# Four seven-product pairs in every gate-and-up group, and bank sums added by transfers

## The chip, the cores and the metric

The kernel runs on one core of one Trainium2 chip. The metric is the device time of one execution in microseconds (us), the median of three runs. The engines are PE (TensorE, matmul; its weight loads are PEld), DVE (VectorE), ACT (ScalarE), POOL (GpSimd) and SP (SyncE, which issues most DMA transfers). Each engine works through its own queue in a fixed order; an instruction that waits holds up what stands behind it on its engine. PE writes to PSUM, eight banks of 128 x 512 fp32; the other memory on the chip is SBUF. A transfer that accumulates reads its destination, adds, and writes it back.

## The reference

One residual block on x of 256 rows and 2048 columns in fp32: a feed-forward half step, a mixing part (gated DeltaNet and attention), and a second feed-forward half step. The change touches only the first two matrix products of both feed-forward parts:

```
def swiglu(h, w_gate, w_up, w_down):
    return (jax.nn.silu(h @ w_gate) * (h @ w_up)) @ w_down

x = x + 0.5 * swiglu(rms_norm(x, ffn1_norm), ffn1_w_gate, ffn1_w_up, ffn1_w_down)
# ... mixing: projections, DeltaNet and attention, gated merge ...
x = x + 0.5 * swiglu(rms_norm(x, ffn2_norm), ffn2_w_gate, ffn2_w_up, ffn2_w_down)
```

Here h is 256 x 2048, w_gate and w_up are 2048 x 5504 and w_down is 5504 x 2048.

## The kernel before

**Precision.** Every fp32 operand is split into a high part (rounded, a cast on ACT) and a low part (the rest, a subtraction on DVE). A product is three matmuls into one bank: high by high, high by low, low by high (`product`, L454 to L456). So each weight tile costs ACT a cast and DVE a subtraction (names `wh`, `wl`; L372 and L426).

**Groups.** The 43 column tiles of the hidden dimension are worked in 11 groups of four tiles (512 columns), the last of three (384). A group is named by its first tile c = 0, 4, ... 40. Eight pairs j = 0 to 7 of 128-row blocks of h are run for each group (`seven`, L480), and give four results: gate and up for both halves of the rows. The groups form three chunks, `CHUNKS`: c = 0 to 12, 16 to 28, 32 to 40. After a chunk comes its down stage, which adds the chunk's part of the third matrix product to x; in the first two chunks this, too, uses seven products for some pairs (`DEEP`).

**Plain and fast pairs.** A plain pair is eight products, 24 matmuls, into four banks: 2, 4, 3, 8. A fast pair computes the same eight from seven products (a Winograd form), 21 matmuls, into seven banks; for it, DVE first forms four combinations of the weight blocks (`s`, L398 to L400), and these are split like weights (`sh`, `sl`), beside two weight blocks `w` and one, `v`. After the last fast pair of a group the seven banks are combined in SBUF into four sums `ev` (tiles `ef`; a copy at L523 and four additions, L524 to L527). The plain banks, which went on collecting, are added to these sums at the end of the group:

```
        for b in (2, 3, 4, 8):
            nc.vector.tensor_add(ev[b], banks[b], ev[b])
```

(L539). Then come SiLU on the two gate sums (ACT, L555) and the product with the two up sums (DVE, L557).

**Which pairs are fast.** FFN 1's group 0 has none. The first two groups of each chunk have four, `FOUR` = 0, 2, 4, 6; the others have three, `FAST` = 0, 2, 4.

**Hidden jobs.** A group's result is transposed on PE (L137) and split (L127 on ACT, L128 on DVE) as two jobs in the following group. In the second to fourth groups of the first two chunks a job may also form the sums for the down stage (tiles `shid`, `hs`; L574, L144 to L147). Jobs are run between plain pairs that come late enough after the last fast one; with `FAST` that is from pair 6 on, with `FOUR` all are left to the end of pair 7.

**Order.** The kernel is written as one program; a scheduler then fixes each engine's order. Weights are fetched by SP some pairs ahead into a heap of 22 SBUF buffers, rounded and split up to a few pairs ahead of PE. Accumulating transfers exist already: the down stage adds its sums to x in DRAM from POOL's queue (L601).

Of the kernel before, what the change touches and what calls it, by code (L numbers as in the profile page):

```python
# [11 lines left out]
F32 = mybir.dt.float32  # L12
F32R = mybir.dt.float32r
AF = mybir.ActivationFunctionType
ALU = mybir.AluOpType
AX = mybir.AxisListType

P = 128
T = 256
D = 2048  # L20
KD = D // P
# [5 lines left out]
BIG = 1e30  # L27
NB = 22
NH = 2
FAST = (0, 2, 4)  # L30
FOUR = (0, 2, 4, 6)
DOWN = (2, 4, 6)
DEEP = (2, 3, 5, 6)
# [2 lines left out]
CHUNKS = ((0, 4), (4, 8), (8, 11))  # L36
# [5 lines left out]
def block_kernel(ctx: ExitStack, tc: tile.TileContext, a: dict, out: bass.AP):  # L42
# [5 lines left out]
    nc = tc.nc  # L48
# [9 lines left out]
    def heap(shape, dt, name):  # L58
        return hp.tile(shape, dt, tag="h", name=name)
# [56 lines left out]
    def tick():  # L116
        for job in later:
            job[0] -= 1
        while later and later[0][0] <= 0:
            later.popleft()[1]()  # L120
# [144 lines left out]
    def fast_pairs(f, i):  # L265
        if f == "1" and i == 0:
            return ()
        return FOUR if any(a0 <= i < a0 + 2 for a0, _ in CHUNKS) else FAST

    def pairs_of(f, i):  # L270
        return FIRST if f == "1" and i == 0 else range(KD // 2)
# [4 lines left out]
    def plan():  # L276

        for f in "12":
            for a0, a1 in CHUNKS:
                for i in range(a0, a1):  # L280
                    c, m = FG[i]
                    js = pairs_of(f, i)
                    gu = zip(*(t_pieces(a[w + f], c, m, 0, KD, [2 * j for j in js]) for w in ("wg", "wu")))
                    for j, p in zip(js, gu):
                        yield j in fast_pairs(f, i), p
                k0, k1 = FG[a0][0], sum(FG[a1 - 1])
                cols = lambda d: t_pieces(a["wd" + f], 4 * d, 4, k0, k1)
                if down_pairs(a0, a1):
                    for d in (0, 2):
                        yield from sevens(cols(d), cols(d + 1), DEEP)  # L290
                else:
                    for d in range(4):
                        yield from twos(cols(d))
            if f == "2":
                return
            yield from mixing()
# [134 lines left out]
    def take_weights():  # L431
        tick()
        while sum(c for c, _ in ready) <= min(PREP, taken[0]) and (left[0] or begun):
            prepare()
        taken[0] += 1
        return ready.popleft()[1]
# [11 lines left out]
    def product(dst, act, wt, start, stop):  # L448

        (ah, al), (wh, wl) = act, wt  # L450
        dst = dst[:, : int(np.prod(wh.shape[1:]))]
        if len(wh.shape) == 3:
            dst = dst.rearrange("p (c x) -> p c x", x=P)
        nc.tensor.matmul(dst, ah, wh, start=start, stop=False)  # L454
        nc.tensor.matmul(dst, ah, wl, start=False, stop=False)  # L455
        nc.tensor.matmul(dst, al, wh, start=False, stop=stop)  # L456
# [20 lines left out]
    def wide(name, n=512):  # L477
        return tp.tile([P, 512], F32, name=name, tag="w", bufs=8)[:, :n]


    def seven(nm, n, fast, act, jobs=(), feed=None, pairs=range(KD // 2), out=None):

        size = {b: len(fast) for b in range(1, 9)}
        for b in (2, 3, 4, 8):
            size[b] += 2 * (KD // 2 - len(fast))
        size[8] -= len(fast)
        done = dict.fromkeys(size, 0)
        banks = {}  # L490

        def add(b, act, wt):
            if b not in banks:
                banks[b] = (acc_bank if b < 5 else core_bank)(f"p{nm}_{b}")[:, :n]
            done[b] += 1
            product(banks[b], act, wt, done[b] == 1, done[b] == size[b])

        ev = {}
        idle = 0
        for at_pair, j in enumerate(pairs):  # L500
            if j in fast:
                ps = take_weights()
                for at, (b, i7, w) in enumerate(ps):
                    add(b, act(j, i7), w)
                    if at == 3:
                        tick()
            else:
                for s in range(2):
                    wh, wl, _ = take_weights()
                    if feed and s == 0:  # L510
                        feed(at_pair)
                    for k, w in enumerate(zip(wh, wl)):
                        for t in range(2):
                            add((2, 4, 3, 8)[2 * s + t], act(j, 2 * k + t), w)
                    idle += 1
                    if idle > 3 and jobs and j > max(fast, default=-1):
                        jobs.popleft()()
                    while at_pair == KD // 2 - 1 and s == 1 and jobs:
                        jobs.popleft()()
            if fast and j == fast[-1]:  # L520
                idle = 1
                g0, u0, g1, u1 = (wide(f"e{nm}_{x}", n) for x in range(4))
                nc.scalar.copy(g0, banks[1])  # L523
                nc.vector.tensor_add(u0, banks[6], g0)  # L524
                nc.vector.tensor_add(g1, banks[7], u0)
                nc.vector.tensor_add(u1, banks[5], g1)
                nc.vector.tensor_add(u0, banks[5], u0)  # L527
                ev = {2: g0, 3: u0, 4: g1, 8: u1}
        if out:
            for b, put in out.items():  # L530
                put(ev[b])
                e = wide(f"e{nm}_{b}", n)
                nc.scalar.copy(e, banks[b])
                put(e)
            return None
        if not fast:
            return banks
        for b in (2, 3, 4, 8):
            nc.vector.tensor_add(ev[b], banks[b], ev[b])  # L539
        return ev  # L540

    def gate_up(nm, f, i, xr, jobs, feed):

        c, m = FG[i]
        n, fast = m * P, fast_pairs(f, i)
        src = seven(f"f{nm}_{c}", n, fast, xr.sums_of, jobs, feed, pairs_of(f, i))
        if not fast:
            banks = src
            src = {b: wide(f"e{nm}_{c}_{b}", n) for b in QUAD}
            for b in QUAD:  # L550
                (nc.scalar.copy if b % 4 else nc.vector.tensor_copy)(src[b], banks[b])
        gs = [src[b] for b in (2, 4)]
        us = [src[b] for b in (3, 8)]
        for t in range(2):
            nc.scalar.activation(gs[t], src[(2, 4)[t]], AF.Silu, scale=xr.rn[:, t : t + 1])  # L555
        for t in range(2):
            nc.vector.scalar_tensor_tensor(  # L557
                us[t], src[(3, 8)[t]], xr.half_rn[:, t : t + 1], gs[t], op0=ALU.mult, op1=ALU.mult
            )
        return us  # L560

    def ffn(nm, xr, nxt, feed):
# [15 lines left out]
        for a0, a1 in CHUNKS:  # L578
# [18 lines left out]
            if fast:  # L597
                block = lambda j, b: act(2 * j + b // 2, b % 2) if b < 4 else [sums[j][:, s, b - 4] for s in range(2)]
                for d in (0, 2):
                    out = {  # L600
                        b: lambda e, dst=xd[d + dd][t]: nc.gpsimd.dma_start(dst, e, accum_op=ALU.add)  # L601
                        for b, (dd, t) in QUAD.items()
                    }
                    seven(f"d{nm}_{a0}{d}", 512, fast, block, out=out)
                continue
# [21 lines left out]
    def put(xs, d):  # L627
        for t in range(2):
            nc.sync.dma_start(xd[d][t], xs[t])
# [506 lines left out]
    def feed(s):  # L1136

        if s < 7:
            xr1.plain(FIRST[s + 1], pair_of_x(FIRST[s + 1]))
        if s < 6:  # L1140
            load_x(2 * FIRST[s + 2], 2)
        if s == 1:
            nc.sync.dma_start(cst, a["cst"])
        if s == 6:
            nc.sync.dma_start(hd, a["hd"].partition_broadcast(P))
        if s > 1 and FIRST[s] in xr1.fast:
            xr1.more(FIRST[s], pair_of_x(FIRST[s]))
        for k4 in range(4):
            if s == max(3, *(FIRST.index(2 * k4 + i) for i in range(2))):
                stand(k4)  # L1150
        if s == 7:
            xr1.finish()
# [49 lines left out]
    act = xr2.more_again(DOWN)  # L1202
# [116 lines left out]
```

## Time and profile before

| | us |
|---|---|
| median of three runs | 2108.11 (2108.03 to 2108.55) |
| the profiled execution | 2107.68 |
| its span, first to last instruction | 2105.9 |
| PE busy | 2090.3 |
| DVE busy | 1767.7 |
| ACT busy | 1179.4 |
| POOL busy | 64.5 |

Rows of groups give line, engine, operation, output and input tile, shapes and count, then busy time and the mean of one. Rows of a timeline give start, duration, engine, line, operation, tiles, count, and in brackets the idle time before with what ended it. A matmul's row lasts longer than the time until the next one starts, since matmuls overlap. A row by stretch of time gives start and end, the length, then the busy time of PE, PEld, DVE, ACT and POOL with counts, the granted clock, the DMA share and GB/s.

### The profile page before, as it was taken

The numbers are of one execution on the slowest core, as the hardware profiler recorded it, in microseconds if no ns is written. First come the engines' busy times: TensorE is split into PE (matmuls) and PEld (weight loads), VectorE is DVE, ScalarE is ACT, GpSimd is POOL, SyncE is SP. The second block draws the span as 40 slices with busy tenths as digits, with TensorE's granted clock in tenths as the row PEclk, the third lists the DMA queues.
The fourth block names the chain that finished last, engine by engine and source line by source line (L and its number), as shares of the span: only waits on it lengthen the run. The fifth ranks groups of instructions, "written<-read, shape, count | busy, mean of one in ns | idle before, by whom it ended". The sixth has DMA issues, their size and how long they took to land.

```text
span 2105.9 us, 25649 instructions
## 1 busy us (share of the span) xinstructions
PE 2090.3 (99%) x9747; PEld 1746.8 (83%) x9747; DVE 1767.7 (84%) x1959; ACT 1179.4 (56%) x1208; POOL 64.5 (3%) x77
## 2 busy tenths in 40 slices
PE   9999999999999999999999999999999999999999
PEld 6888888878898988888888888888887888878897
DVE  6998999989996788667784787669999999989982
ACT  6755565645655555567555554555555555556561
POOL 0000110002000000000010000000000100011000
PEclk9999999999999999999999999999999999999999
DMA  9655995649866656435454467757665975579581
GB/s 317 219 189 175 262 265 196 205 145 278 253 217 211 237 197 219 164 120 200 145 180 160 142 204 231 234 179 230 202 198 167 280 238 196 180 206 295 186 272 60
DMA packets 398202, 434.57 MB, mean 206 GB/s; under 512 B 14704, under 2 KB 372352, under 8 KB 397824
## 3 DMA queue, kind: packets, MB, share of 16 engines
q1 hardware_dynamic: 388864, 416.17, 60.9%
q0 software_dynamic: 9216, 16.78, 4.5%
q8 instruction: 76, 1.25, 0.2%
q14 instruction: 46, 0.38, 0.1%
HBM read 407.72 MB, written 25.17 MB: 206 GB/s over the span
## 4 chain that ended last, share of the span: by engine, by line
PE 96%; DVE 2%; SPq 1%; issue 0%; DMA 0%; ACT 0%; DVEq 0%; ACTq 0%
PE pf L454 14%; PE pf L456 14%; PE pf L455 14%; PE pd L455 7%; PE pd L456 7%; PE pd L454 7%; PE pg L455 2%; PE pg L456 2%; PE pg L454 2%; PE pc L454 2%; PE pc L456 2%; PE pc L455 2%; PE pwo L456 1%; PE pwo L454 1%; PE pwo L455 1%; DVE wl L426 1%
## 5 line engine op out<-in xcount | busy, mean ns | idle before, releaser
L426 DVE TENSOR_TENSOR wl<-raw,wh 128x2048 fp32r<-128x2048 f32 (+5 forms) x283 | 598.7, 2125 | 70.5 <-PE pc L455 16.9
L372 ACT CAST wh<-raw 128x2048 fp32r<-128x2048 f32 (+5 forms) x283 | 499.9, 1782 | 95.7 <-DVE wl L426 20.5
L405 ACT CAST sh<-s 128x2048 fp32r<-128x2048 f32 (+1 forms) x118 | 223.4, 1893 | 279.5 <-DVE s L400 276.5
L426 DVE TENSOR_TENSOR sl<-s,sh 128x2048 fp32r<-128x2048 f32 (+1 forms) x118 | 265.8, 2258 | 26.8 <-PE pd L455 11.9
L455 PE MATMUL pf<-wl,xr 128*128 128x512 f32 (+1 forms) x704 | 271.4, 386 | 0.0
L456 PE MATMUL pf<-wh,xr 128*128 128x512 f32 (+1 forms) x704 | 271.3, 385 | 0.0
L454 PE MATMUL pf<-wh,xr 128*128 128x512 f32 (+1 forms) x704 | 262.2, 387 | 2.2 <-ACT xr L179 1.5
L456 PE MATMUL pd<-wh,hid 128*128 128x512 f32 x432 | 169.1, 391 | 0.0
L455 PE MATMUL pd<-wl,hid 128*128 128x512 f32 x432 | 168.3, 389 | 0.0
L454 PE MATMUL pd<-wh,hid 128*128 128x512 f32 x432 | 163.6, 392 | 0.0
L403 ACT CAST w<-raw 128x1024 fp32r<-128x1024 f32 (+1 forms) x118 | 122.8, 1040 | 64.7 <-DVE sl L426 12.8
L454 PEld LDWEIGHTS pf<-wh,xr 128*128 128x128 f32 x704 | 132.7, 189 | 28.3 <-ACT xr L179 1.9
L456 PEld LDWEIGHTS pf<-wh,xr 128*128 128x128 f32 x704 | 132.5, 188 | 25.4 <-DVE xr L180 0.2
L455 PEld LDWEIGHTS pf<-wl,xr 128*128 128x128 f32 x704 | 132.6, 188 | 25.2 <-DVE wl L426 0.4
L426 DVE TENSOR_TENSOR w<-raw,w 128x1024 fp32r<-128x1024 f32 (+1 forms) x118 | 142.3, 1206 | 10.1 <-ACT w L403 9.9
L398 DVE TENSOR_TENSOR s<-raw 128x1024 f32<-128x1024 f32 (+1 forms) x118 | 142.1, 1204 | 6.8 <-PE pg L455 4.6
L403 ACT CAST v<-raw 128x512 fp32r<-128x512 f32 (+1 forms) x118 | 72.6, 615 | 91.3 <-PE pf L456 30.9
L455 PE MATMUL pf<-sl,xf 128*128 128x512 f32 (+1 forms) x296 | 113.8, 385 | 0.0
L456 PE MATMUL pf<-sh,xf 128*128 128x512 f32 (+1 forms) x296 | 113.5, 385 | 0.0
L454 PE MATMUL pf<-sh,xf 128*128 128x512 f32 (+1 forms) x296 | 112.0, 386 | 0.0
L601 POOL DMA_DIRECT2D xd<-ed x64 | 56.0, 997 | 1305.7 <-ACT ed L523 1228.1
L456 PEld LDWEIGHTS pd<-wh,hid 128*128 128x128 f32 x432 | 81.1, 188 | 17.2
(472 smaller groups left out, 4247.9 us busy)
## 6 DMA issues: line engine op xcount, KB each, us to landing
raw<-wd SPq DMA_DIRECT2D x168, 512.0 KB, 5.1
raw<-wg SPq DMA_DIRECT2D x159, 512.0 KB, 3.8
raw<-wu SPq DMA_DIRECT2D x159, 512.0 KB, 5.2
raw<-wgt SPq DMA_DIRECT2D x64, 512.0 KB, 4.6
raw<-wa SPq DMA_DIRECT2D x48, 512.0 KB, 4.6
raw<-wc SPq DMA_DIRECT2D x48, 512.0 KB, 4.6
xd<-ed POOLq DMA_DIRECT2D x64, 256.0 KB, 6.9
raw<-wbr SPq DMA_DIRECT2D x32, 512.0 KB, 4.9
```

Of the source, the lines that this page charges most:

```text
L372: nc.scalar.copy(hi, src)
L398: nc.vector.tensor_sub(S[:, 0:2], R[:, 1], R[:, :, 0])
L403: nc.scalar.copy(hi, src)
L405: nc.scalar.copy(sh, s)
L426: nc.vector.tensor_sub(lo, src, f32(hi))
L454: nc.tensor.matmul(dst, ah, wh, start=start, stop=False)
L455: nc.tensor.matmul(dst, ah, wl, start=False, stop=False)
L456: nc.tensor.matmul(dst, al, wh, start=False, stop=stop)
L601: b: lambda e, dst=xd[d + dd][t]: nc.gpsimd.dma_start(dst, e, accum_op=ALU.add)
```

## The change

All groups but FFN 1's group 0 now have four fast pairs. That concerns the third and fourth group of the first two chunks and the last group, ten in all (c = 8, 12, 24, 28, 40 in both FFNs). In all groups with fast pairs but a chunk's last one, the additions of L539 are no longer made: ACT copies the four plain banks into a new SBUF tile `es`, in the order 2, 4, 3, 8, and POOL issues a transfer for each that adds it to the sum `ev`. These are 15 groups: c = 4, 8, 16, 20, 24, 32, 36 in FFN 1 and the same with c = 0 in FFN 2. SiLU and the product with the up sums now follow the transfers.

```diff
-FAST = (0, 2, 4)
 FOUR = (0, 2, 4, 6)
...
         if f == "1" and i == 0:
             return ()
-        return FOUR if any(a0 <= i < a0 + 2 for a0, _ in CHUNKS) else FAST
+        return FOUR
...
-    def seven(nm, n, fast, act, jobs=(), feed=None, pairs=range(KD // 2), out=None):
+    def seven(nm, n, fast, act, jobs=(), feed=None, pairs=range(KD // 2), out=None, spill=False):
...
         if not fast:
             return banks
+        if spill:
+            es = heap([P, 4, n], F32, f"e{nm}")
+            for i, b in enumerate((2, 4, 3, 8)):
+                nc.scalar.copy(es[:, i], banks[b])
+                nc.gpsimd.dma_start(ev[b], es[:, i], accum_op=ALU.add)
+            return ev
         for b in (2, 3, 4, 8):
             nc.vector.tensor_add(ev[b], banks[b], ev[b])
         return ev
...
         n, fast = m * P, fast_pairs(f, i)
-        src = seven(f"f{nm}_{c}", n, fast, xr.sums_of, jobs, feed, pairs_of(f, i))
+        spill = all(i != a1 - 1 for _, a1 in CHUNKS)
+        src = seven(f"f{nm}_{c}", n, fast, xr.sums_of, jobs, feed, pairs_of(f, i), spill=spill)
```

In the changed kernel the lines up to the new branch stand one lower in number, and behind it higher: the bank copy is L540, its transfer L541, SiLU L561, the product L563, and DVE's split L425.

The orders show what moves. First, ACT at the end of FFN 1's group 20 (the second group of a chunk), before. `ef1_20` are the group's sums, `pf1_20` its banks (the number behind is the bank), `hid1_4` the hidden tile of the group ahead of it. The number in `wh67` counts weight pieces: 66 is pair 2 of the next group, 67 its pair 3, 68 its pair 4:

```order
L405 CAST sh66_2792<-s66_2784 128x2048
L127 CAST hid1_4_2514<-hid1_4_2514_0_0_2808 128x2x256
L127 CAST hid1_4_2514<-hid1_4_2514_2_0_2815 128x2x256
L555 ACTIVATE ef1_20_0_2751<-ef1_20_0_2751,rn1_106 128x512
L372 CAST wh67_2863<-raw67_2760 128x2048
L555 ACTIVATE ef1_20_2_2753<-ef1_20_2_2753,rn1_106 128x512
L403 CAST v68_2886<-raw68_2781 128x512
L403 CAST w68_2885<-raw68_2781 128x1024
L405 CAST sh68_2892<-s68_2884 128x2048
```

And in the changed kernel:

```order
L404 CAST sh66_2821<-s66_2813 128x2048
L126 CAST hid1_4_2543<-hid1_4_2543_0_0_2837 128x2x256
L126 CAST hid1_4_2543<-hid1_4_2543_2_0_2844 128x2x256
L540 COPY ef1_20_2851<-pf1_20_2_2548 128x512
L540 COPY ef1_20_2851<-pf1_20_4_2560 128x512
L540 COPY ef1_20_2851<-pf1_20_3_2568 128x512
L540 COPY ef1_20_2851<-pf1_20_8_2611 128x512
L371 CAST wh67_2897<-raw67_2789 128x2048
L561 ACTIVATE ef1_20_0_2780<-ef1_20_0_2780,rn1_106 128x512
L561 ACTIVATE ef1_20_2_2782<-ef1_20_2_2782,rn1_106 128x512
L402 CAST w68_2919<-raw68_2810 128x1024
L402 CAST v68_2920<-raw68_2810 128x512
```

ACT now makes four copies between the hidden tile and pair 3's rounding, and both SiLUs stand together behind that rounding, ahead of all of pair 4.

DVE at the same place, before:

```order
L539 TENSOR_TENSOR ef1_20_0_2751<-pf1_20_2_2519,ef1_20_0_2751 128x512
L426 TENSOR_TENSOR wl65_2764<-raw65_2682,wh65_2763 128x2048
L128 TENSOR_TENSOR hid1_4_2514<-hid1_4_2514_0_0_2808,hid1_4_2514 128x2x256
L128 TENSOR_TENSOR hid1_4_2514<-hid1_4_2514_2_0_2815,hid1_4_2514 128x2x256
L539 TENSOR_TENSOR ef1_20_1_2752<-pf1_20_3_2539,ef1_20_1_2752 128x512
L539 TENSOR_TENSOR ef1_20_2_2753<-pf1_20_4_2531,ef1_20_2_2753 128x512
L539 TENSOR_TENSOR ef1_20_3_2754<-pf1_20_8_2582,ef1_20_3_2754 128x512
L557 SCALAR_TENSOR_TENSOR ef1_20_1_2752<-ef1_20_1_2752,rh1_107,ef1_20_0_2751 128x512
L557 SCALAR_TENSOR_TENSOR ef1_20_3_2754<-ef1_20_3_2754,rh1_107,ef1_20_2_2753 128x512
L426 TENSOR_TENSOR w66_2785<-raw66_2703,w66_2785 128x1024
L426 TENSOR_TENSOR v66_2786<-raw66_2703,v66_2786 128x512
L426 TENSOR_TENSOR sl66_2793<-s66_2784,sh66_2792 128x2048
```

And in the changed kernel:

```order
L425 TENSOR_TENSOR v66_2815<-raw66_2732,v66_2815 128x512
L127 TENSOR_TENSOR hid1_4_2543<-hid1_4_2543_0_0_2837,hid1_4_2543 128x2x256
L127 TENSOR_TENSOR hid1_4_2543<-hid1_4_2543_2_0_2844,hid1_4_2543 128x2x256
L425 TENSOR_TENSOR sl66_2822<-s66_2813,sh66_2821 128x2048
L397 TENSOR_TENSOR s68_2918<-raw68_2810 128x1024
L563 SCALAR_TENSOR_TENSOR ef1_20_1_2781<-ef1_20_1_2781,rh1_107,ef1_20_0_2780 128x512
L563 SCALAR_TENSOR_TENSOR ef1_20_3_2783<-ef1_20_3_2783,rh1_107,ef1_20_2_2782 128x512
L398 TENSOR_TENSOR s68_2918<-s68_2918,raw68_2810 128x512
L425 TENSOR_TENSOR w68_2919<-raw68_2810,w68_2919 128x1024
L399 TENSOR_TENSOR s68_2918<-raw68_2810,s68_2918 128x512
L425 TENSOR_TENSOR v68_2920<-raw68_2810,v68_2920 128x512
L425 TENSOR_TENSOR wl67_2898<-raw67_2789,wh67_2897 128x2048
```

The additions are gone, pair 2's `w` and `v` have moved ahead of the hidden tile, and the product with the up sums now stands behind the first difference of pair 4 (`s68`), with the rest of pair 4 and pair 3's `wl67` behind it.

Last, ACT at the end of FFN 1's group 24 (the third group of a chunk), where the sums for the down stage are made, in the changed kernel:

```order
L126 CAST hid1_5_2864<-hid1_5_2864_0_0_3159 128x2x256
L126 CAST hid1_5_2864<-hid1_5_2864_2_0_3174 128x2x256
L580 COPY shid1_5_2864_0_3166<-hid1_5_2864_0_0_3159 128x128
L580 COPY shid1_5_2864_2_3181<-hid1_5_2864_2_0_3174 128x128
L126 CAST hs1_52_2865<-shid1_5_2864_0_3166 128x512
L540 COPY ef1_24_3189<-pf1_24_2_2870 128x512
L540 COPY ef1_24_3189<-pf1_24_4_2882 128x512
L540 COPY ef1_24_3189<-pf1_24_3_2890 128x512
L126 CAST hs1_52_2865<-shid1_5_2864_2_3181 128x512
L540 COPY ef1_24_3189<-pf1_24_8_2933 128x512
L371 CAST wh75_3235<-raw75_3111 128x2048
L561 ACTIVATE ef1_24_0_3102<-ef1_24_0_3102,rn1_106 128x512
```

The first copy stands behind the rounding of the first `hs` tile, which is made from DVE's differences; the fourth stands behind the second. Before, the two jobs of this group lay at pairs 6 and 7, ahead of its end. On PE, 14 products of the next group's pairs 0 and 2 stand ahead of the first that needs bank 2.

## The prediction

> **What bounds the kernel now.** I read the page first: its head, the busy table, the clock row, the chain of waits.
>
> ```profile
> span 2105.9 us, 25649 instructions
> PE 2090.3 (99%) x9747; PEld 1746.8 (83%) x9747; DVE 1767.7 (84%) x1959; ACT 1179.4 (56%) x1208; POOL 64.5 (3%) x77
> ...
> PEclk9999999999999999999999999999999999999999
> ...
> q0 software_dynamic: 9216, 16.78, 4.5%
> ...
> PE 96%; DVE 2%; SPq 1%; issue 0%; DMA 0%; ACT 0%; DVEq 0%; ACTq 0%
> ...
> xd<-ed POOLq DMA_DIRECT2D x64, 256.0 KB, 6.9
> ```
>
> PE is the bound: 96% of the chain, at an undisturbed clock. What PE does not compute is a gain, as long as the weights (ACT rounds the high part, DVE subtracts the low part) and the banks arrive in time. How near DVE is to failing that is read from the busy times by stage: the groups of FFN 1's second chunk, its down stage, and the short group.
>
> ```profile
> 300.00:350.00 50.00, 50.00 (x222) 41.39 (x222) 49.32 (x48) 28.60 (x24) 0.00 (x0) 1.00 0.65 214
> 350.00:395.00 45.00, 45.00 (x208) 37.31 (x207) 42.71 (x49) 25.97 (x25) 0.00 (x0) 1.00 0.51 165
> 395.00:437.00 42.00, 42.00 (x191) 34.78 (x190) 37.47 (x33) 22.75 (x20) 0.00 (x0) 1.00 0.62 201
> 437.00:553.00 116.00, 115.07 (x510) 94.08 (x509) 109.54 (x108) 67.33 (x63) 13.95 (x16) 1.00 0.85 245
> 600.00:635.00 35.00, 35.00 (x204) 34.18 (x203) 29.64 (x32) 19.80 (x20) 0.00 (x0) 1.00 0.83 263
> ```
>
> The third number is DVE, the fourth ACT, the last but one the DMA share. Where four pairs go by seven products (300 to 350) DVE has 0.7 us free in 50; where three do (395 to 437), 4.5 in 42. So 84% over the span says little: in these groups DVE is almost a second bound, and any wait put into its queue can reach PE.
>
> **The gain.** Ten groups get a fourth fast pair, 21 matmuls in place of 24. PE's order has 9372 rows before and 9342 after, so 30 matmuls go: 24 of 512 columns and 6 of 384 (the short group of each FFN). Matmuls overlap, so their price is the distance of their starts.
>
> ```profile
> 351.50 0.39 PE L454 MATMUL pf<-wh,xr 128*128 128x512 f32 x1
> 351.73 0.39 PE L455 MATMUL pf<-wl,xr 128*128 128x512 f32 x1
> 351.96 0.40 PE L456 MATMUL pf<-wh,xr 128*128 128x512 f32 x1
> 352.19 1.04 PE L137 MATMUL hid<-cst,ef 128*128 128x128 f32 x8
> 352.98 0.47 PE L454 MATMUL pf<-w,xf 128*128 128x512 f32 x1
> ...
> 612.14 0.33 PE L454 MATMUL pf<-wh,xr 128*128 128x384 f32 x1
> 612.32 0.33 PE L455 MATMUL pf<-wl,xr 128*128 128x384 f32 x1
> ```
>
> 24 x 0.227 + 6 x 0.173 = **6.5 us**, the most that leaves PE.
>
> **DVE and ACT work.** The rows of DVE at the end of group 20 of FFN 1 (T = 352.19, the first transpose after the last product) price everything.
>
> ```profile
> 345.71 0.68 DVE L524 TENSOR_TENSOR ef<-pf,ef 128x512 f32<-128x512 f32 x1
> 346.31 1.21 DVE L398 TENSOR_TENSOR s<-raw 128x1024 f32<-128x1024 f32 x1
> ...
> 350.44 0.68 DVE L539 TENSOR_TENSOR ef<-pf,ef 128x512 f32<-128x512 f32 x1
> 351.04 2.28 DVE L426 TENSOR_TENSOR wl<-raw,wh 128x2048 fp32r<-128x2048 f32 x1
> 353.44 1.29 DVE L128 TENSOR_TENSOR hid<-hid,hid 128x512 fp32r<-128x512 f32 x2
> 354.65 1.88 DVE L539 TENSOR_TENSOR ef<-pf,ef 128x512 f32<-128x512 f32 x3
> 356.44 1.40 DVE L557 SCALAR_TENSOR_TENSOR ef<-ef,rh,ef 128x512 f32<-128x512 f32 x2
> 357.76 1.22 DVE L426 TENSOR_TENSOR w<-raw,w 128x1024 fp32r<-128x1024 f32 x1
> 358.90 0.69 DVE L426 TENSOR_TENSOR v<-raw,v 128x512 fp32r<-128x512 f32 x1
> ...
> 365.78 2.28 DVE L426 TENSOR_TENSOR wl<-raw,wh 128x2048 fp32r<-128x2048 f32 x1
> 367.99 2.29 DVE L426 TENSOR_TENSOR sl<-s,sh 128x2048 fp32r<-128x2048 f32 x1
> ```
>
> By the distance of starts: 512 columns 0.60, 1024 columns 1.14, 2048 columns 2.2 us. A fast pair costs DVE 1.14 + 0.6 + 0.6 + 1.14 + 0.6 + 2.2 = 6.3, a plain one 2.2: 4.1 more for each of ten pairs, 41 us (less in the short groups). Four additions (L539) fall away in 15 groups: 60 x 0.60 = 36 us. Over the span DVE is even. In the last group of a chunk, which keeps its additions, DVE gets 4.1 us more in the 4.5 that the row 395 to 437 leaves; I take 0 for that, and up to 2 us for each of four such groups if its free time lies badly (the short groups have room). ACT gets 60 copies, with 19 to 21 us free in each of the first three stretches. Neither costs anything in itself. SP's rows are as many as before, and POOL is idle in these stretches. Sixty more transfers of 256 KB beside the 64 there (4.5% of the DMA engines) add 4.2%, where a third or more is free.
>
> **The new wait.** In front of the sums now stands a transfer. ACT's order at the end of group 20 is: two roundings of the hidden tile, four copies, one weight rounding (pair 3's high part), then SiLU on the first two sums, which waits for the first two landings. DVE's is: low part of pair 2, first difference of pair 4, then L563, which waits for the third and fourth landing. Queued behind it: the rest of pair 4's differences, its two low parts, and pair 3's low part, which PE needs. POOL's rows of the accumulating transfers that are there already (to DRAM, same size) price a landing.
>
> ```profile
> L601 POOL DMA_DIRECT2D xd<-ed x1: 862/862/862, 262.0 to 262.0; - x1
> DMA to landing us min/median/max: 4.3/4.3/4.3
> ...
> L601 POOL DMA_DIRECT2D xd<-ed x3: 865/1216/1569, 527.5 to 528.5; - x3
> DMA to landing us min/median/max: 6.7/7.9/9.1
> ```
>
> One alone lands 4.3 us after its issue. Three issued 0.54 us apart land 6.7, 0.54 + 7.9 = 8.4 and 1.07 + 9.1 = 10.2 after the first issue: 1.75 each further on. The fourth of four thus lands, after the first issue, at 4.3 + 3 x 1.2 = 8.0 if a quiet queue starts them 1.2 apart (my estimate: two thirds of the loaded spacing), or at 10.2 + 1.75 = 12.0 as in the loaded stage. The DMA share here is 0.5 to 0.65, there 0.85, and weight loads come in bursts, so I take **9.0**, nearer the quiet end.
>
> [...] The trace has 4.3 at best and a median of 6.9 on the page for the same size, so I go by the rows. [...]
>
> Second groups of a chunk (c = 4, 20, 36 in both FFNs: six). ACT's row gives the first copy:
>
> ```profile
> 352.83 1.07 ACT L127 CAST hid<-hid 128x512 fp32r<-128x512 f32 x2 [0.30 <-PE hid L137]
> 353.79 0.74 ACT L555 ACTIVATE ef<-ef,rn 128x512 f32<-128x512 f32 x1
> ...
> L523 ACT COPY ef<-pf x21: 482/582/587, 91.1 to 2020.4; 128x512 f32<-128x512 f32 x19, 128x384 f32<-128x384 f32 x2
> ```
>
> ACT is free at T + 1.6, the first copy (582 ns in the row of L523) ends at T + 2.2, its transfer issues at T + 2.3; the fourth lands at T + 11.3 (10.3 to 14.3). DVE, with the additions gone and pair 2's w and v ahead of the hidden tile, goes 350.44 + 2.2 + 1.14 + 0.6 + 1.2 + 2.2 + 1.14 = 358.9 = T + 6.7 and stands there. From the last landing: L563 0.7, then 0.6 + 1.14 + 0.6 + 0.6 + 2.28 = 5.2: pair 3's low part is done at T + 17.2 (16.2 to 20.2). PE wants it after the transposes (0.8), 21 + 24 + 21 products x 0.227 and one more: T + 16.0. So PE waits **1.2 us** (0.2 to 4.2). Times six: 7.2 (1.2 to 25).
>
> First groups (c = 16, 32, and c = 0 in FFN 2: five). No hidden tile stands ahead, but pair 2's rounding does, which waits for DVE: about T + 0.1. First copy T + 0.7, last landing T + 9.8 (8.8 to 12.8), low part T + 15.7, wanted at T + 15.2: **0.5** (0 to 3.5). Times five: 2.5 (0 to 18).
>
> Third groups (c = 8, 24 in both: four), with the rows of such sums:
>
> ```profile
> L144 DVE TENSOR_TENSOR shid<-shid,hid x16: 276/281/290, 136.9 to 1852.8; 128x128 f32<-128x128 f32 x16
> ...
> L127 ACT CAST hs<-shid x16: 614/620/624, 139.0 to 1853.8; 128x512 fp32r<-128x512 f32 x16
> ```
>
> With four fast pairs the hidden jobs all come at the group's end, and here they make the sums for the down stage: DVE subtracts twice and forms the first four differences, ACT rounds them, and only then copies. DVE reaches them at T + 2.3 (350.44 + 2.2 + 1.14 + 0.6 = 354.4, as above), so: 1.2 + 4 x 0.2 + 0.62 for ACT's rounding + 0.58, first copy T + 5.5. PE has 14 products between the transposes and its first use of bank 2, to T + 4.0: a wait of 1.5 (0.5 if DVE is on time). Last landing T + 14.6, low part T + 20.5, wanted at T + 17.5: 3.0 more. Together **4.5**; 7.5 at 12 us a landing, 2.4 at 8 us and with DVE on time (first copy T + 4.4). Times four: 18 (10 to 30).
>
> **Sum**, against the profiled execution's own 2107.68 (span 2105.9 and 1.8 around it; the median of the runs, 2108.11, is 0.4 higher): 7.2 + 2.5 + 18 = 27.7 lost, 6.5 won: +21, or **2129**. Lower bounds: 1.2 + 0 + 10 - 6.5 = +5, 2112. Upper: 25 + 18 + 30 + 8 (last groups) - 6.5 = +75, 2182.
>
> **The rivals.**
> *The gain is kept (faster).* If the fourth landing comes before about 8 us after the first issue, the second and first groups lose nothing, since DVE has 36 us less to do just there; if it is 6 us or less, L563 in the third groups finds it done as well. For it: the lone transfer of 4.3, destination in SBUF rather than DRAM, a DMA share of 0.5. Against: four come together, and the loaded rows. Result 2107.7 - 6.5 = 2101, up to 2103 with some of the bank waits left. Chance 0.24.
> *Cancelled.* The quiet bound everywhere: waits of 3 to 11 us, 2104 to 2112. Chance 0.13.
> *DVE becomes the bound.* At 12 us each stop costs DVE some 7 us in groups where it has 1 to 3 free, and the bound of each of the 15 ends is reached: above 2152, towards 2182. For it: the loaded rows were measured with this very kind of transfer. Against: the DMA share. Chance 0.08.
> That the change does not do what it says is excluded by the 30 rows.
>
> **How the numbers follow.** My forecast, waits of 11 to 51 us against 6.5 won, 2112 to 2152, has 0.55. The time is its centre, 2129. About 0.2%, 4.2 us, can be told from no change: below 2103.9 is faster, 0.24; to 2112.3 the same, 0.13; above, slower, 0.63. The range from 2101 to 2152 leaves out the last rival and a gain above 6.5, some 0.11; the forecast's own is 2112 to 2152.
>
> **What would show it.** In the profile after: L563 among DVE's waits, put down to the transfer into ef, 2 to 6 us each, 15 times, and L561 among ACT's; PE waiting on the low part (L425) and, in the third groups, on copies (L540); landings of ef of 5 to 9 us in the median; DVE busy for about as long as before. Wrong: landings near 3 us and no such waits, with PE's time down by 6.5; or PE's losses lying in the last groups and down stages, where I take nothing.

## The result, and the profile after

The changed kernel takes **2212.5 us** in the median of five runs (2212.16 to 2216.03), the kernel before 2108.11, also of five (2107.50 to 2108.55): a ratio of 1.0495, 95% interval 1.0483 to 1.0507. It is slower by 104.4 us. The prediction was 2129, with a range from 2101 to 2152: the direction was right, the size wrong by a factor of five.

From the page of the changed kernel (the columns are those of the page before; the line of L563 has busy time, mean ns, then the idle time ahead of it and what ended it):

```profile
span 2210.7 us, 25852 instructions
...
PE 2119.8 (96%) x9717; PEld 1759.8 (80%) x9717; DVE 1771.3 (80%) x1949; ACT 1224.2 (55%) x1288; POOL 117.5 (5%) x137
...
q0 software_dynamic: 17856, 32.51, 8.8%
...
L563 DVE SCALAR_TENSOR_TENSOR ef<-ef,rh,ef 128x512 f32<-128x512 f32 (+1 forms) x42 | 30.7, 735 | 102.0 <-DMA ef<-ef 102.0
```

and from its view of waits (who waits for whom: us in total, times, longest):

```profile
DVE ef L563 <- DMA ef<-ef: 102.0, 30, 7.4
PE pf L454 <- DVE wl L425: 69.2, 16, 7.0
ACT ef L561 <- DMA ef<-ef: 53.9, 26, 4.0
...
PE pf L453 <- ACT ef L540: 0.8, 1, 0.8
```

VectorE (DVE) is as busy as before (1767.7 then), but stands 102 us at the product with the up sums. That is 6.8 us at each of the 15 transferred groups. Behind each stop PE waits for a low part. How one stop looks shows in the timeline at the end of FFN 1's group 16, the first of its chunk (start, us, engine, line, operation; in brackets the idle time before). First GpSimd (POOL), with the four issues:

```profile
327.89 3.53 POOL L541 DMA_DIRECT2D ef<-ef  x4 [34.47 <-ACT ef L540]
```

Then ScalarE (ACT) in the same timeline, the two SiLUs:

```profile
332.72 0.72 ACT L561 ACTIVATE ef<-ef,rn 128x512 f32<-128x512 f32 x1 [1.84 <-DMA ef<-ef]
337.18 0.72 ACT L561 ACTIVATE ef<-ef,rn 128x512 f32<-128x512 f32 x1 [3.74 <-DMA ef<-ef]
```

And VectorE, from the last work ahead of the product to pair 3's low part:

```profile
331.18 1.21 DVE L397 TENSOR_TENSOR s<-raw 128x1024 f32<-128x1024 f32 x1
339.00 0.75 DVE L563 SCALAR_TENSOR_TENSOR ef<-ef,rh,ef 128x512 f32<-128x512 f32 x1 [6.61 <-DMA ef<-ef]
340.78 0.75 DVE L563 SCALAR_TENSOR_TENSOR ef<-ef,rh,ef 128x512 f32<-128x512 f32 x1 [1.03 <-DMA ef<-ef]
...
344.39 2.28 DVE L425 TENSOR_TENSOR wl<-raw,wh 128x2048 fp32r<-128x2048 f32 x1
```

The chain is the one the prediction drew: copies, four transfers, L563, the rest of pair 4, then pair 3's low part, done at 346.7, which PE wanted at 342.0. What differs is the time of the last landing, 340.78: 12.9 us after the first issue, where 9.0 was taken. So it is at all 15. I measured the start of the second L563 from the first issue, and PE's wait as the distance of two matmul starts beyond the usual one (0.227 us at 512 columns):

| groups | last landing after first issue: predicted, measured (mean) | PE's wait each: predicted, measured |
|---|---|---|
| first (5) | 9.0; 12.1 to 13.4 (12.8) | 0.5; 4.4 to 7.1 (5.3) |
| second (6) | 9.0; 10.1 to 11.3 (10.7) | 1.2; 2.4 to 4.9 (3.5) |
| third (4) | 9.0; 11.5 to 12.8 (11.9) | 4.5; 5.5 to 6.8 (6.0) |

These waits sum to 71 us. PE also ran slowly behind them. The same stretch in the view by windows, changed kernel (the fifth engine is POOL, then the granted clock, the DMA share and GB/s):

```profile
327.90:340.80 12.90, 12.90 (x58) 10.70 (x57) 5.26 (x6) 5.88 (x8) 3.53 (x4) 1.00 0.96 225
342.00:347.00 5.00, 0.40 (x2) 0.27 (x2) 5.00 (x6) 3.09 (x2) 0.00 (x0) 0.89 1.10 350
347.00:352.00 5.00, 5.00 (x12) 3.86 (x13) 5.00 (x5) 2.07 (x3) 0.00 (x0) 0.50 0.10 31
```

From 347 to 352 the granted clock is 0.50 and PE makes 12 products in 5 us, their starts 0.43 us apart; ahead of the wait, at a clock of 1.00, they are 0.227 apart, 22 in 5 us. The trace has such half-speed windows of 3.4 or 6.8 us behind 14 of the 15 waits. Summed over the kernel, the distances between matmul starts beyond the usual ones grow by 111 us: 82 in gaps over 0.35 us (the 15 waits, the gap right behind most of them and a few short waits) and 29 in the small ones, some 27 of them in the half-speed stretches. Less the 6.5 us that PE saves, that is the 104.8 us by which the span grew.

By stage: the six stretches of gate and up groups are 13.1, 19.1, 12.4, 22.4, 18.2 and 13.6 us longer than before (98.8), the four down stages of the full chunks 2.3, 1.2, 1.1 and 1.0 (5.6).

### The profile page after: what moved, and what is told of

Its sections match the earlier page's. It is cut to its first block, busy times and chain, and to the rows that moved or that the text cites. A ratio compares the mean times of both kernels' runs of the same rounds, so it can differ in the third digit from the quotient of the medians.

```text
span 2210.7 us, 25852 instructions
## 1 busy us (share of the span) xinstructions
PE 2119.8 (96%) x9717; PEld 1759.8 (80%) x9717; DVE 1771.3 (80%) x1949; ACT 1224.2 (55%) x1288; POOL 117.5 (5%) x137
## 5 line engine op out<-in xcount | busy, mean ns | idle before, releaser
L425 DVE TENSOR_TENSOR wl<-raw,wh 128x2048 fp32r<-128x2048 f32 (+5 forms) x273 | 576.9, 2122 | 85.7 <-PE pf L454 19.2
L371 ACT CAST wh<-raw 128x2048 fp32r<-128x2048 f32 (+5 forms) x273 | 483.5, 1782 | 94.1 <-DVE wl L425 22.0
L404 ACT CAST sh<-s 128x2048 fp32r<-128x2048 f32 (+1 forms) x128 | 241.5, 1886 | 326.3 <-DVE s L399 323.0
L454 PE MATMUL pf<-wl,xr 128*128 128x512 f32 (+1 forms) x704 | 285.9, 406 | 69.2 <-DVE wl L425 69.2
L425 DVE TENSOR_TENSOR sl<-s,sh 128x2048 fp32r<-128x2048 f32 (+1 forms) x128 | 287.3, 2250 | 21.2 <-PE pd L454 11.2
L455 PE MATMUL pf<-wh,xr 128*128 128x512 f32 (+1 forms) x704 | 281.4, 400 | 0.0
L453 PE MATMUL pf<-wh,xr 128*128 128x512 f32 (+1 forms) x704 | 277.0, 399 | 3.8 <-ACT xr L178 2.4
L425 DVE TENSOR_TENSOR w<-raw,w 128x1024 fp32r<-128x1024 f32 (+1 forms) x128 | 153.8, 1201 | 5.9 <-ACT w L402 5.2
L453 PE MATMUL pf<-sh,xf 128*128 128x512 f32 (+1 forms) x336 | 128.0, 387 | 2.0 <-DVE shid L146 2.0
L455 PE MATMUL pf<-sh,xf 128*128 128x512 f32 (+1 forms) x336 | 129.1, 384 | 0.0
L454 PE MATMUL pf<-sl,xf 128*128 128x512 f32 (+1 forms) x336 | 129.0, 384 | 0.0
L563 DVE SCALAR_TENSOR_TENSOR ef<-ef,rh,ef 128x512 f32<-128x512 f32 (+1 forms) x42 | 30.7, 735 | 102.0 <-DMA ef<-ef 102.0
L541 POOL DMA_DIRECT2D ef<-ef x60 | 53.1, 1353 | 1013.4 <-ACT ef L540 684.5
```

The source lines that it names most:

```text
L371: nc.scalar.copy(hi, src)
L404: nc.scalar.copy(sh, s)
L425: nc.vector.tensor_sub(lo, src, f32(hi))
L541: nc.gpsimd.dma_start(ev[b], es[:, i], accum_op=ALU.add)
L563: nc.vector.scalar_tensor_tensor(us[t], src[(3, 8)[t]], xr.half_rn[:, t : t + 1], gs[t], op0=ALU.mult, op1=ALU.mult)
```

## The experiments

Theory L says that the landings, through VectorE's stop, make the loss. Rival D says that the fourth fast pair fills VectorE and is to blame with or without transfers. Rival C says that the transfers crowd out the weight loads.

### Each part of the change alone

**Four fast pairs, no transfer.**

```
-        spill = all(i != a1 - 1 for _, a1 in CHUNKS)
+        spill = False
```

> Four fast pairs in all groups, but the plain banks are added by VectorE in every group, as before: no transfer at all. Theory L (the wait of VectorE for the last landing is what costs): no landing, no wait; the 6.5 us that PE saves less some 0 to 10 us of VectorE's 41 us of extra work, 2101 to 2112, and no half-speed stretches. Rival D (the fourth fast pair fills VectorE, and the low parts come late with or without transfers): above 2130.

Measured: 2120.5 us, ratio 1.0054 (1.0039 to 1.0069): between the two ranges.

**The transfers alone.**

```
-        return FOUR
+        return FOUR if any(a0 <= i < a0 + 2 for a0, _ in CHUNKS) else FAST
```

> The transfers in the same 15 groups, but the fast pairs as before (three in the last groups of the first two chunks and wherever the kernel before had three). Theory L: the stops are where they were, 15 of 3.5 to 6 us with 1 to 2.5 us of half-speed matmuls behind each, and 41 us of VectorE's work less changes little, since VectorE stands still in that time anyway: 2190 to 2215. Rival D: most of the loss is gone, below 2150.

Measured: 2199.7 us, 1.0430 (1.0414 to 1.0446). The two parts add up: 12.3 + 91.5 = 103.8 us of the 104.4. D falls, and the transfers are nearly nine tenths of the loss. VectorE stops as long (100.4 us) although it has 37 us less work (1734.3 us busy in place of 1771.3). But the four pairs miss theory L's range too. Without a transfer they should have won 6.5 us and lose 12.3; more on that below.

### The wait or the traffic

**No transfers, copies kept.**

```
-                nc.gpsimd.dma_start(ev[b], es[:, i], accum_op=ALU.add)
```

> The changed kernel without its 60 transfers; the copies by ScalarE stay. Leaves out the plain banks' part of the sums in 15 groups. Theory L: 2100 to 2106, no waits for the low parts. Rival D, or a rival in which the copies or the moved hidden jobs cost: above 2130.

Measured: 2114.8 us, 1.0026 (1.0016 to 1.0037). This is 9 us above theory L's range and far below D's. L's other half holds: PE's wait for the low part, 69.2 us in the changed kernel, is 0.2. Where the 9 us lie is taken up below.

**Transfers that nobody reads.**

```
-                nc.gpsimd.dma_start(ev[b], es[:, i], accum_op=ALU.add)
+                nc.gpsimd.dma_start(es[:, i], es[:, i], accum_op=ALU.add)
```

> The 60 transfers add into the copy's own tile, which nobody reads: the same bytes on the same queue at the same places, but nothing waits for a landing. Leaves out the plain banks' part of the sums in 15 groups. Theory L: 2100 to 2110, as without transfers. Rival C (the transfers crowd the weight loads out of the DMA engines, and raw weights come late): a large part of the 104 us stays, above 2140.

Measured: 2124.4 us, 1.0077 (1.0060 to 1.0094), above theory L's range and below C's. The kernel with the transfers running is 9.7 us slower than without; waiting for them costs the other 88. The landings are as late as in the changed kernel (the last one 9.8 to 12.8 us after the first issue), so it is the waiting that is gone, not the lateness. C explains a tenth. And not all of that is traffic. From the view of waits of the unread run:

```profile
ACT sh L404 <- DMA ef<-ef: 25.9, 4, 7.6
...
ACT wh L371 <- DMA ef<-ef: 18.0, 7, 4.6
```

ScalarE's roundings wait for a landing although they read nothing of it. The copy's tile is one of the 22 buffers of the heap, and so are the tiles that these roundings write; that a rounding got the copy's buffer and had to wait until its transfers had landed is read from the program, not tested by a run. It is a second way in which a landing is waited for, and the prediction did not have it. The changed kernel's view of waits has no such line.

### Who waits, and for how many

**Two transfers in place of four** (`es` then has two slots).

```
-            for i, b in enumerate((2, 4, 3, 8)):
+            for i, b in enumerate((3, 8)):
                 nc.scalar.copy(es[:, i], banks[b])
                 nc.gpsimd.dma_start(ev[b], es[:, i], accum_op=ALU.add)
+            for b in (2, 4):
+                nc.vector.tensor_add(ev[b], banks[b], ev[b])
```

> Two transfers in place of four: banks 3 and 8 (up) go by ScalarE's copy and a transfer as in the changed kernel, banks 2 and 4 (gate) are added by VectorE as before. Theory L: the second landing comes some 6 to 8 us after the first issue, where the fourth came at 10 to 13; most of the low parts are in time then, and VectorE has 18 us more work: 2120 to 2150, mean wait below 1.5 us. Rival F (a landing has a fixed price that does not depend on the transfers in flight): above 2170.

Measured: 2147.3 us, 1.0182 (1.0161 to 1.0202). Theory L's range is met, F's is not. The second product starts 5.8 to 9.5 us after the first issue, 7.5 in the mean, and in the view of waits VectorE's stop is less than half, PE's wait less than a third:

```profile
DVE ef L565 <- DMA ef<-ef: 45.9, 27, 4.3
...
PE pf L454 <- DVE wl L425: 21.9, 14, 5.0
```

**Four transfers of half the bytes.**

```
-                nc.gpsimd.dma_start(ev[b], es[:, i], accum_op=ALU.add)
+                nc.gpsimd.dma_start(ev[b][:, : n // 2], es[:, i, : n // 2], accum_op=ALU.add)
```

> The changed kernel with the same 60 transfers at the same places, but each moves the first half of the columns only (128 KB in place of 256; 96 in the short groups). Leaves out half of the plain banks' part of the sums in 15 groups. Theory B (a landing is set by the bytes that the transfers and the weight loads put through the DMA engines): the fourth landing comes at 7 to 8.5 us after the first issue in place of 10 to 13, and the time is near that with two whole transfers, 2130 to 2155. Rival F (a fixed price for each transfer in the queue, whatever its size): the fourth landing stays at 10 or more, above 2180.

Measured: 2174.2 us, 1.0305 (1.0288 to 1.0321): between the two, and neither is right. The second product starts 7.3 to 10.8 us after the first issue, 9.5 in the mean. VectorE's stop at it has two main parts, the second of them behind ScalarE's SiLU:

```profile
DVE ef L563 <- DMA ef<-ef: 46.4, 21, 5.9
...
DVE ef L563 <- ACT ef L561: 20.2, 5, 5.7
```

With 11.7 for four whole ones and 7.5 for two, three points give: halving the bytes at the same number takes 2.2 us off, halving the number at the same bytes 2.0. So bytes and number count about equally, some 1.0 us for each transfer and 1.1 for each 256 KB, on some 3 that are there anyway. That is three numbers from three points, so nothing here tests it.

**The product on GpSimd, so that VectorE waits for no landing.**

```
+            if spill:
+                nc.gpsimd.tensor_scalar(us[t], src[(3, 8)[t]], xr.half_rn[:, t : t + 1], None, op0=ALU.mult)
+                nc.gpsimd.tensor_mul(us[t], us[t], gs[t])
+                continue
             nc.vector.scalar_tensor_tensor(
```

> The four transfers stay, but the product with the up sums goes from VectorE to GpSimd (two operations each, scale and multiply), so VectorE never waits for a landing; ScalarE's SiLU still waits for the first two, ahead of pair 4's roundings. Theory L: VectorE's stop is what costs; what is left is the second landing (6 to 9.3 us after the first issue) that holds ScalarE and through pair 4's low parts VectorE: 1 to 3 us in the first groups, near none elsewhere, 2122 to 2150. Rival S (ScalarE's stop alone is enough): above 2170.

Measured: 2173.1 us, 1.0302 (1.0287 to 1.0318). Theory L's number is missed and S's is met, but that does not show S. First its view of waits:

```profile
DVE w L425 <- ACT w L402: 64.3, 23, 6.7
ACT ef L561 <- DMA ef<-ef: 58.6, 26, 5.0
```

VectorE still stands 64.3 us, now for the rounded parts that are queued behind ScalarE's SiLU. In the changed kernel the two stops lie in the same time, so one of them hides the other. So far this is S. But the run has a second price, which neither theory names. Busy time of the engines, and one group of VectorE's instructions, first in the changed kernel, then here:

```profile
PE 2119.8 (96%) x9717; PEld 1759.8 (80%) x9717; DVE 1771.3 (80%) x1949; ACT 1224.2 (55%) x1288; POOL 117.5 (5%) x137
L425 DVE TENSOR_TENSOR sl<-s,sh 128x2048 fp32r<-128x2048 f32 (+1 forms) x128 | 287.3, 2250 | 21.2 <-PE pd L454 11.2
...
PE 2108.0 (97%) x9717; PEld 1746.1 (80%) x9717; DVE 1796.3 (83%) x1917; ACT 1221.9 (56%) x1288; POOL 305.3 (14%) x201
L425 DVE TENSOR_TENSOR sl<-s,sh 128x2048 fp32r<-128x2048 f32 (+1 forms) x128 | 301.6, 2361 | 23.3 <-PE pd L454 11.1
```

VectorE has 32 instructions fewer, the products, which took 0.75 us each, and is busy 25 us longer: its other instructions last some 49 us more in all, nearly all of it (45 us) in the 132 during which GpSimd computes. So this edit takes 24 us of products off VectorE and puts 49 us of slower work on it. Of the 59 us by which its span is longer than that of the run without transfers, 25 are busy time of VectorE and 34 are idle time. How much ScalarE's stop alone would cost is not shown.

**GpSimd adds, no transfer.**

```
-                nc.gpsimd.dma_start(ev[b], es[:, i], accum_op=ALU.add)
+                nc.gpsimd.tensor_add(ev[b], es[:, i], ev[b])
```

> No transfer: ScalarE copies the plain banks as in the changed kernel, and GpSimd adds the copies to the sums, an operation of 128x512 each. Theory L: if GpSimd makes the four in under 6 us (no row of the traces shows its price), nothing waits long, and the time is that of the run without transfers, 2112 to 2122; at 2 us each the last sum comes at 8 to 9 us and some of the waits return: to 2150. Rival D: as for the run without transfers.

Measured: 2152.2 us, 1.0203 (1.0186 to 1.0220), just above the upper end. First the group of GpSimd's additions, then VectorE's wait for them:

```profile
L541 POOL TENSOR_TENSOR ef<-ef,ef 128x512 f32<-128x512 f32 x60 | 83.1, 1415 | 960.4 <-ACT ef L540 960.4
```

```profile
DVE ef L563 <- POOL ef L541: 41.9, 15, 3.7
```

No transfer at all, and still a loss, as VectorE stops for 2.8 us at each of 15 groups. Here, too, VectorE's instructions got slower: 1949 of them take 1788.4 us, in place of 1771.4 in the run without transfers. Set side by side, against that run (2114.8 us, VectorE idle for 341 us of its span; the kernel before was 2108.2 to 2109.0 beside these runs, so the second column is good to about 1 us):

| run | VectorE's stop at that place, us | time above 2114.8 | VectorE's busy time above | its idle time above |
|---|---|---|---|---|
| changed kernel | 102.0 | 97.7 | 0 | 98 |
| four half transfers | 69.8 (46.4 for landings, the rest behind ScalarE) | 59.4 | 0 | 60 |
| two transfers | 45.9 | 32.5 | 16 (30 additions) | 13 |
| GpSimd adds | 41.9 | 37.4 | 17 | 23 |
| product on GpSimd | 64.3 (behind ScalarE) | 58.4 | 25 | 34 |
| unread | none at that place | 9.7 | -1 | 10 |

The last two columns are of the profiled executions, and add up to the growth of the span by definition. What they show is where the stop went. **In the two runs in which VectorE has the same work as without transfers, 0.85 to 0.96 us of the kernel go for each microsecond in which it stands**: it makes up little elsewhere. In the next three the loss is mixed with more busy time of VectorE, and of the shorter stops a good part is made up: with two transfers it stops for 45.9 us and is idle for only 13 us more in all. So "no free time" holds for the long stops, not for every microsecond.

The table alone can't tell this from an account by PE. PE's waits for the low part are 69.2, 38.9, 21.9 and 25.8 us in the first four rows, and 1.4 to 1.5 us of the kernel go for each microsecond of them; what comes on top of the wait could be VectorE's arrears or the half speed behind it. The next two runs are about that.

### Is the half speed a price of its own?

**16 matmuls on zeros put into PE's wait**, ahead of the first product of pair 3 (the tile `zr` holds zeros, so the sum does not change):

```
+                    if fill and at_pair == 3 and s == 0:
+                        for _ in range(16):
+                            nc.tensor.matmul(banks[2], zr, wh[0], start=False, stop=False)
```

> The changed kernel with 16 more matmuls, on a tile of zeros, in each of the 15 groups that follow a transferred one, directly ahead of the first product of pair 3, whose low part comes late. They add zeros to the same bank: 16 x 0.227 = 3.6 us of PE each, 54 in all, put where PE waits 2.4 to 7 us. Theory H (an idle PE falls to half speed for the 1 to 5 us behind the wait, and this is some 27 us of the loss): the low part comes when it came, the matmuls are free where the wait is longer than 3.6, and the half-speed windows shrink: 2185 to 2210. Rival N (the half speed has another cause, and the fill is paid in part): 2213 to 2267.

Measured: 2210.8 us, 1.0482 (1.0466 to 1.0497), between the two ranges. The fill did what it was for. From 346 to 352, where the clock was 0.50, it is now full (view by windows):

```profile
346.00:352.00 6.00, 5.55 (x25) 4.25 (x24) 6.00 (x5) 3.92 (x4) 0.00 (x0) 1.00 0.50 157
```

The half-speed windows sum to 19 us of the trace in place of 81 (mean granted clock 0.996 in place of 0.982). In the view of waits PE's 69.2 us for the low part are 15.6:

```profile
PE pf L456 <- DVE wl L427: 15.6, 12, 2.6
PE pd L455 <- DVE ef L549: 9.4, 4, 3.8
```

The time did not follow. The group stretches are 16 us shorter and the down stages 16 longer; the second line is one of the waits there, for the last groups' sums. So I filled only the 9 groups that are not the last of a chunk (the cut is against the run above):

```
-        fill=all(i != a0 for a0, _ in CHUNKS) and (f, i) != ("1", 1)
+        fill=all(i not in (a0, a1 - 1) for a0, a1 in CHUNKS) and (f, i) != ("1", 1)
```

> As the kernel with 16 zero matmuls ahead of pair 3, but only in the 9 groups that follow a transferred one and are not the last of their chunk, so that the down stages start as in the changed kernel. The fill covers 3.6 us of each wait; the half-speed stretch behind these 9 (some 1.7 us of PE each, 15 in all) goes. Theory H (the half speed is a price of its own): 2194 to 2204. Rival A (VectorE's arrears set the time whatever PE's speed: what PE gains behind the wait it waits for later): 2208 to 2216.

Measured: 2213.4 us, 1.0494 (1.0479 to 1.0508). Half-speed windows 48 us in place of 81 (mean granted clock 0.989), and nothing won: rival A's number. Part of this is the fill's own doing. Behind three second groups the changed kernel's wait was shorter than 3.6 us, by some 2.5 us in all, and waits of 0.3 to 0.9 us appear at the next group ends, where PE now arrives ahead of VectorE's sums and of the hidden tile. That the half-speed stretches cost 27 us on top is therefore not shown. It agrees better with both runs that PE is slow in a time in which VectorE is catching up anyway. How much of the 27 is left as a price of its own stays open.

### Where the fourth pair's gain went

In the run without transfers the group stretches differ from before by +0.1, -0.7, -0.3, -0.8, -0.8 and -0.3 us, in place of the 6.5 us that fewer matmuls allow, and the four down stages are 5.1, 1.2, 1.7 and 1.4 us longer. Two runs on the kernel before, one for the last groups and one for the others:

```
-        return FOUR if any(a0 <= i < a0 + 2 for a0, _ in CHUNKS) else FAST
+        return FAST if FG[i][0] in (8, 24, 40) else FOUR
```

> The kernel before with the fourth fast pair in the last groups of the first two chunks alone (c = 12 and 28, both FFNs); all additions by VectorE, no transfer. PE saves 4 x 0.7 = 2.7 us. Theory P (VectorE's work on the last groups' fourth pair reaches into the down stage, whose first weights then come late; the down stages were 9 us longer in the runs without transfers): 2111 to 2116. Rival Q (the down stage is late because of the hidden jobs that the third groups have moved to their end): below 2108.

Measured: 2111.6 us, 1.0009 (1.0001 to 1.0018), 2.6 us above the kernel before in the same runs and so just clear of it. The groups win 0.9 to 1.5 us in each chunk, and the down stages lose 2.6, 1.0, 1.3 and 1.4. Q's number is excluded and P's is met, and the view of waits has a line that the kernel before has not, for a low part in the down stage. It covers 3.0 of the 6.3 us.

```profile
PE pd L455 <- DVE wl L426: 3.0, 4, 1.7
```

The other run:

```
+        return FAST if FG[i][0] in (12, 28) else FOUR
```

> The kernel before with the fourth fast pair in the third groups (c = 8 and 24) and the short group (c = 40) of both FFNs alone; all additions by VectorE, no transfer. PE saves 4 x 0.7 + 2 x 0.5 = 3.8 us. Theory P: the down stages are as before, and waits of about 1 us at the entry of the third groups' successors eat part of it: 2104 to 2109. Rival Q: the down stages are longer, above 2112.

Measured: 2120.6 us, 1.0051 (1.0037 to 1.0065). Q's number, but not Q's place: the down stages are as before (0 to 1 us), and the groups of the full chunks lose 3.3 to 5.5 us each (in the profiled execution, which at 2125.1 us was the slowest of the five). Its view of waits:

```profile
PE pf L454 <- ACT sh L405: 11.8, 6, 2.5
```

In a third group with four fast pairs the hidden jobs come at the group's end, on top of the additions, and the next group's sums of weights (`sh`) come late. Four of the six waits, 2.5 us each, are at the entry of the third groups' successors: the place that theory P named, at about 1 us.

**The version that these runs point to**: the fourth pair in the short group alone, where each run without transfers had won something.

```
+        return FOUR if i == len(FG) - 1 or any(a0 <= i < a0 + 2 for a0, _ in CHUNKS) else FAST
```

> The kernel before with the fourth fast pair in the short group (c = 40) of both FFNs alone, nothing else changed. PE saves 6 matmuls of 384 columns, 6 x 0.173 = 1.0 us; the last chunk's groups were 0.3 to 0.6 us shorter in each run without transfers. If that holds: 2107.0 to 2107.8 against 2108.2, at the edge of what can be told; rival: its VectorE work reaches into the last down stage as it does in the full groups, 2109 to 2112.

Measured: 2107.7 us, ratio 0.9995 (0.9986 to 1.0004). The trace has the 0.6 us in each of the two short chunks, but the time can't be told from the kernel before. No version was found that is faster by a measurable amount.

## Why the prediction was right and wrong

**The chain of waits: right.** L563 waits for transfers and L561 with it, PE waits on L425, and VectorE is as busy as before. The median landing is 7.6 us, in the 5 to 9 that were named. L563's waits were put at 2 to 6 us for each group and are 6.8 in the mean, above that.

**The landing: mis-sized.** 9.0 us was taken between bounds of 8.0 and 12.0, and 11.7 is the mean of 15, from 10.1 to 13.4. The first step that failed is "Sixty more transfers of 256 KB ... add 4.2%, where a third or more is free". That is an average over the span, and the transfers come in 15 bursts. In the stretch of a burst the DMA share is 0.96 in the row above (behind group 16). Behind group 20 it was 0.35 before the change and is 0.89 after it:

```profile
352.20:364.00 11.80, 11.80 (x58) 9.89 (x57) 11.68 (x14) 6.01 (x8) 0.00 (x0) 1.00 0.35 109
...
377.80:387.90 10.10, 10.10 (x45) 8.32 (x45) 4.14 (x4) 5.89 (x8) 3.53 (x4) 1.00 0.89 208
```

What the page gives would have told it. The software queue takes 8.8% of 16 engines over 2210.7 us for 124 transfers, 25 us of engine time each, or 1.6 us of all sixteen (1.5 from the 4.5% and 64 transfers of the page before). Four need an estimated 6.3 us of every DMA engine, beside weight loads that take 0.35 (the first row) to 0.65 (the prediction's first) of them. The quiet bound of 8.0 could hardly be met.

**From the landing to PE's wait: right.** With the measured landings the prediction's own arithmetic gives 5 x 4.25 + 6 x 2.9 + 4 x 7.4 = 68 us against the 71 measured. Part of that agreement is luck: the first and second groups come out 1.1 and 0.6 short, the third ones 1.4 long, as their bank wait (1.5 each) hardly came, 0.8 once. So the mis-sized landing is worth 68 - 27.7 = 40 of the 83 us by which 2129 was short.

**What the sum ended at: wrong.** This is the second step that failed, and it has the other 43 us. The sum counted one late low part for each stop and let VectorE be "even over the span", so it had no term for what follows the wait. It had itself read that VectorE has 0.7 us free in 50. Counted on VectorE, the long stops are paid almost in full: 15 x 6.8 = 102 us, less the 2.8 by which the group stretches are shorter without transfers, plus the 5.6 in the down stages, is the 104.8 of the span. Counted on PE, the same time is 71 us of waits, 11 in other gaps and 29 in small ones, less 6.5. The fill runs speak for the first count, as PE without most of the half speed won nothing; how much of it is a price of its own stays open. The third rival, "DVE becomes the bound", had the mechanism and even "each stop costs DVE some 7 us". It got 0.08, as I read the DMA share against it. Its price ended at 2182, as it was taken from the same sum over late low parts; 15 times its own 7 us, less the 6.5 won, would have given 2207.

**The last groups and down stages: taken at 0, up to 8 us.** Measured: 5.6 us in the down stages of the changed kernel and 9.4 without transfers. The last groups' run supports the cause that theory P gives, and has a wait for about half of it. The third groups' moved jobs, priced only as a later first copy, cost 3.3 to 5.5 us for each full chunk when the additions stay on VectorE.

**The gain: right as a count, never reached as time.** The 30 matmuls went, but the group stretches of the run without transfers are only 2.8 us shorter.

**The other two rivals** needed landings near 6 or 8 us. None of 15 came before 10.1. A single one of the 60 transfers landed 3.4 us after its own issue at the shortest, and 7.6 in the median.

## What to carry to other kernels

Price a new wait by what the waiting engine has free in that stretch: where it has next to nothing, a long stop is paid almost one for one (here 0.85 to 0.96 us for each microsecond), also if the engine that you look at has slack at the first place where the lateness shows. Price a burst of transfers in its own stretch, by engine time for each transfer from the queue's share beside the share that the stretch has already, never by the share over the span. A tile that a transfer still reads can hold its buffer, as the unread run suggests (25.9 and 18.0 us of ScalarE's waits): look who gets that buffer next. And where a run moves work to an idle engine to test a wait, compare the busy times of the others as well: here VectorE's instructions got slower beside GpSimd's (by 49 us with the product there, by 17 us with the additions).

## What the runs showed of the hardware

In the changed kernel PE fell to half speed (granted clock 0.50) behind a wait, in windows of 3.4 or 6.8 us: behind 14 of the 15 waits, down to one of 2.35 us (group 20 of FFN 1), while one of 2.61 us (group 20 of FFN 2) had none.

GpSimd added 128x512 floats in 1.42 us in the mean, where VectorE's distance of starts is 0.60. In the run with the product there, its multiplication of two tiles took 2.0 us, and that by a column of scalars 3.4. VectorE's instructions got longer while GpSimd computed: with the additions there the products of L563 took 1148 ns for 512 columns in place of 749, and with the product there the low parts `sl` took 2384 ns for 2048 columns in place of 2283.
